# Expert rows of two mixture layers: loads before the last two experts, one-hot products for those two, transposes late in the products before

## The chip, the cores and the metric

The kernel runs on one core of a Trainium2 chip. The metric is the device time of one execution in microseconds (us). Three runs of the kernel before took 1920.16 to 1924.55 us, with a median of 1920.88 us.

## The reference, cut to what matters

The model is two blocks one after the other. The first is a state-space and attention block with a feed-forward part; the second has two layers, each a mixer (gated linear attention in layer 0, sparse attention in layer 1) followed by a mixture of experts. The change lies in the mixture of experts of both layers and in the layer normalization behind it:

```python
def moe_ffn(x, w_router, b_router, w_gate, w_up, w_down):
    ...
    s = jax.nn.sigmoid((xt @ w_router).astype(jnp.float32))
    ...
    _, top_e = lax.top_k(jnp.where(in_grp, biased, NEG), TOP_K)
    w = jnp.take_along_axis(s, top_e, axis=-1)
    w = w / jnp.sum(w, axis=-1, keepdims=True)
    gate = jnp.zeros((n, N_EXPERTS), jnp.float32).at[...].set(w)
    h = jax.nn.silu(jnp.einsum('nd,edf->nef', xt, w_gate)) * jnp.einsum('nd,edf->nef', xt, w_up)
    h = h * gate[:, :, None].astype(h.dtype)
    return jnp.einsum('nef,efd->nd', h, w_down).reshape(B, S, D)
...
    f = moe_ffn(x, moe_w_router, moe_b_router, moe_w_gate[i], moe_w_up[i], moe_w_down[i])
    x = layer_norm(DN_ALPHA * x + f, ln_g[i, 1], ln_b[i, 1])
```

There are 512 tokens of 1024 features, 16 experts with 256 hidden features each, and every token goes to two experts. Each expert has 3 MB of weights, so a layer reads 48 MB.

## The kernel before, in words

Tensors of tokens lie as four tiles of 128 tokens, xt[0] to xt[3], with 1024 features each. A product in nearly full precision is made as three products of halves (mm3, lines 393 to 396): every operand is split into a high part, cast on ScalarE, and the rest, subtracted on VectorE (split, line 368).

Weights come through one stream of 1 MB tiles (class Stream, lines 318 to 349). get asks for the load of a tile where the tile is used in program order, and rotates through a ring of buffers, ten (WM) in the expert layers. The framework then orders each engine's instructions by a simulated time line: a load whose buffer is free is issued long ahead of its use, in the order in which instructions become ready. An edge made by after (line 313) says that one instruction stands behind another on its engine, without a semaphore; Stream.later (line 341) gives every load of the stream such an edge behind the instruction st.behind, where that is set. All loads named here are issued by the queue of SyncE, SP, in which one that waits holds up what stands behind it.

```python
def ahead(self, n):
    for i in range(self.used, min(self.used + n, len(self.src))):
        if i not in self.tiles:
            ...
            ld = nc.sync.dma_start(out=t[:, :ap.shape[1]], in_=ap)
            self.later(ld)
def later(self, ld):
    if self.behind is not None:
        after(ld, self.behind)
def get(self):
    self.ahead(1)
```

Only project (line 1282) asks for ten tiles at once, before the experts begin. Of the 48 tiles of a layer the order is two of gate and up weights for expert e, then the one of down weights for expert e - 1.

The experts of a layer (experts, line 1463) run in a loop of 17 steps. Step e issues the gather of expert e + 1's rows from the DRAM copy xd of the tokens (gather, line 1423: an indirect DMA by GpSimd into one of three buffers xg, then eight transposes into PSUM tile xgt and a split into gh and gl, two buffers each), then the products of expert e with gate and up weights (up, line 1436: 24 matmuls into psh, two weight tiles), then those of expert e - 1 with its down weights (down, line 1445: two transposes ht, 12 matmuls into psy, one weight tile; ScalarE copies psy to SBUF, GpSimd scatters the rows to the DRAM tensor yd, one row for each token and choice).

combine (line 1480) follows. Eight loads of 512 KB bring yd back in the order of tokens, each behind all 16 scatters; st.behind is then set to the last of them. For each tile VectorE adds both choices, weighted (mac, line 1497, L1502), takes the statistics (L1512 to L1520), and ScalarE normalizes (L1173); done works on the tile before. In layer 0 done is x4_tile: transposes, split, and the products n with the weights w1, whose three tiles are split after the last psy is copied (line 1640). In layer 0 the first choice of tile 3 is weighted on ScalarE and added on GpSimd (aside). In layer 1 done is finish: gain and bias on GpSimd and VectorE and the store to the output. VectorE's order in this part is that of the program.

Of the kernel before, what the change touches and what calls it, by code (L numbers as in the profile page):

```python
# [10 lines left out]
F32 = mybir.dt.float32  # L11
FR = mybir.dt.float32r
F16 = mybir.dt.float16
# [6 lines left out]
P = 128  # L20
D = 1024
KD = 8
# [246 lines left out]
def build(ctx, tc, I, out, dbg=None):  # L269
# [123 lines left out]
    def mm3(o, a, b, start, stop):  # L393
        TE.matmul(o, a[0], b[0], start=start, stop=False)  # L394
        TE.matmul(o, a[0], b[1], start=False, stop=False)  # L395
        TE.matmul(o, a[1], b[0], start=False, stop=stop)  # L396

# [759 lines left out]
    def load_gb(gi):  # L1157
        gb = [sb(1024, n) for n in ("lng", "lnb")]
# [27 lines left out]
    class Layer:  # L1186
# [115 lines left out]
        def slots(self, q, idx):  # L1302

            psi = p1("inv")
            for i, (k, t) in enumerate(q):
                TE.matmul(psi[:, :32], q[k, t], self.rr[:, k, t], start=i == 0, stop=i == 7)
            return V.tensor_scalar(idx, psi[:, :32], float(2 * S), None, op0=ALU.add)

        def route(self, ts):
# [42 lines left out]
            self.idx = small("idx", (32,), I32)  # L1352
            wt.behind = self.slots(self.q, self.idx).ins.name

        def token_weights(self):
# [15 lines left out]
            V.reciprocal(wss, wss)  # L1371
            tt(self.wts, self.wts, wss.unsqueeze(1).to_broadcast([P, 2, 4]), ALU.mult)

        def overflow(self):

            top = nc.values_load(self.cnt[0:1, 0:1], min_val=0, max_val=S)
            with tc.If(top > CAP):
# [3 lines left out]
                with tc.For_i(1, S // P, 1):  # L1381
# [3 lines left out]
                    with tc.For_i(0, 16, 1) as e:  # L1385
# [27 lines left out]
                        for k in range(2):  # L1413
                            for nh in range(2):
# [3 lines left out]
                        A.copy(v2(yo), psy)  # L1418
                        G.indirect_dma_start(out=self.yd, out_offset=bass.IndirectOffsetOnAxis(ap=ie[:, 1:2], axis=0),
                                             in_=yo, in_offset=None, bounds_check=2 * S - 1, oob_is_err=False)  # L1420
            drop("oxg", "oxT", "ow", "ohs", "oyo", "qoh")

        def gather(self, e):
            xg = self.xg[e % 3]
            ld = G.indirect_dma_start(out=xg, out_offset=None, in_=self.xd, in_offset=bass.IndirectOffsetOnAxis(ap=self.idx[:, e:e + 1], axis=0),  # L1425
                                      bounds_check=S - 1, oob_is_err=False)
            if e == 0:
                st.hold = {st.used + WM + i: ld.ins.name for i in range(2)}
            ps = p2("xgt")
# [15 lines left out]
        def down(self, e, hs):  # L1445
# [10 lines left out]
            self.last = A.copy(v2(yo), psy).ins.name  # L1456
            s = G.indirect_dma_start(out=self.yd, out_offset=bass.IndirectOffsetOnAxis(ap=self.idx[:, 16 + e:17 + e], axis=0),
                                     in_=yo, in_offset=None, bounds_check=2 * S - 1, oob_is_err=False)
            for o in self.scat:
                tc.declare_no_dep(s.ins, o.ins, reason="rows of another expert's tokens")  # L1460
            self.scat.append(s)

        def experts(self):
            drop("zT", "lng", "lnb")
            wt.bufs = 4
            self.scat = []
            g, hs = {0: self.gather(0)}, {}
# [12 lines left out]
        def combine(self, done, aside):  # L1480

            ydv = self.yd.rearrange("(a k) d -> a k d", k=2)
            y2 = {}
            for t in range(4):
                for k in range(2):
                    y2[t, k] = sb(1024, "y2", bufs=8)
                    ld = nc.sync.dma_start(out=y2[t, k], in_=ydv[t * P:(t + 1) * P, k])
                    for s in self.scat:
                        tc.add_manual_dep(ld.ins, s.ins.name, mybir.DependencyInfo(mybir.DependencyClass.Sync, mybir.DependencyReason.DATA),
                                          reason="the rows of every expert")  # L1490
# [6 lines left out]
            def mac(t, k):  # L1497
                if k == 0 and t in aside:
                    A.activation(y2[t, 0], y2[t, 0], AF.Copy, scale=self.wts[:, 0, t:t + 1])
                    tt(xt[t], xt[t], y2[t, 0], ALU.add, G)  # L1500
                else:
                    V.scalar_tensor_tensor(xt[t], y2[t, k], self.wts[:, k, t:t + 1], xt[t], op0=ALU.mult, op1=ALU.add)  # L1502

            with tc.manual_schedule(engines={mybir.EngineType.DVE}):
                mac(0, 0)
                for t in range(5):
                    if t < 4:
                        z = xt[t]
                        mac(t, 1)
                        bs, mv, rs = (small(n, (w,), bufs=2) for n, w in (("bs", 12), ("mv", 2), ("lrs", 2)))  # L1510
# [12 lines left out]
                    if t < 4:  # L1523
                        normalize(z, z, rs)
            drop("y2")

# [81 lines left out]
    L0 = Layer(0)  # L1608
    L0.start()
    todo = [(f, b) for f in (gla_scores, gla_keys, gla_states) for b in range(4)]  # L1610
    for m in range(8):
# [63 lines left out]

    L0.combine(x4_tile, (3,))
    drop("x4f")
# [40 lines left out]
    for t in range(4):  # L1718
        affine(xt[t], L0.gb, V)
        dump(f'x4_{t}', xt[t])  # L1720
    drop("lng", "lnb")
    o = stream_tm(x4a)
# [200 lines left out]
    L1 = Layer(1)  # L1923
    L1.start()

    todo = [(i, [h]) for i in (3, 2) for h in range(16)] + [(i, [h, h + 1]) for i in (1, 0) for h in range(0, 16, 2)]
# [51 lines left out]
    def finish(t):  # L1978
# [4 lines left out]
        nc.sync.dma_start(out=out[t * P:(t + 1) * P, :], in_=xt[t])  # L1983
    L1.combine(finish, ())

# [15 lines left out]
```

## Time and profile before

| | us |
|---|---|
| median of three runs | 1920.88 |
| profiled execution, device time | 1918.51 |
| its span from first to last instruction | 1916.7 |
| layer 0: first gathered row transposed / last psy ends / layer's normalization begins | 1096.8 / 1255.9 / 1267.8 |
| layer 1: the same three | 1706.1 / 1871.7 / 1883.2 |

The span is counted from the first instruction; times in the rows are from there. PE is the matmul engine, DVE VectorE, ACT ScalarE, POOL GpSimd, SP the queue of loads and stores. In brackets behind an instruction stands how long its engine was idle before it and what ended that.

### The profile page before, as it was taken

The numbers are of one execution on the slowest core, as the hardware profiler recorded it, in microseconds if no ns is written. First come the engines' busy times: TensorE is split into PE (matmuls) and PEld (weight loads), VectorE is DVE, ScalarE is ACT, GpSimd is POOL, SyncE is SP. The second block draws the span as 40 slices with busy tenths as digits, with TensorE's granted clock in tenths as the row PEclk, the third lists the DMA queues.
The fourth block names the chain that finished last, engine by engine and source line by source line (L and its number), as shares of the span: only waits on it lengthen the run. The fifth ranks groups of instructions, "written<-read, shape, count | busy, mean of one in ns | idle before, by whom it ended". The sixth has DMA issues, their size and how long they took to land.

```text
span 1916.7 us, 27254 instructions
## 1 busy us (share of the span) xinstructions
PE 1743.3 (91%) x10719; PEld 1480.1 (77%) x10719; DVE 1221.8 (64%) x2276; ACT 874.1 (46%) x1397; POOL 173.3 (9%) x140
## 2 busy tenths in 40 slices
PE   8999999899999999999999799949998999859990
PEld 7899877798989988877888578738886777647870
DVE  7855368776555643253347889874337777669985
ACT  4233346433333332243223288843236665628881
POOL 2310000022000000000000122110000000012213
PEclk9999999899999999999999799979898999879995
DMA  5335221242322233212225599752230003539953
GB/s 194 110 110 140 89 88 65 63 160 90 108 89 89 88 135 114 95 66 88 88 88 206 188 325 380 281 217 77 85 136 23 1 12 123 208 126 338 380 224 140
DMA packets 69205, 269.73 MB, mean 141 GB/s; under 512 B 22144, under 2 KB 24720, under 8 KB 44240
## 3 DMA queue, kind: packets, MB, share of 16 engines
q1 hardware_dynamic: 52384, 246.38, 35.9%
q0 software_dynamic: 9216, 16.80, 2.4%
q10 hardware_dynamic: 7472, 4.76, 1.2%
q8 instruction: 85, 1.39, 0.3%
q14 instruction: 48, 0.39, 0.1%
HBM read 249.62 MB, written 30.43 MB: 146 GB/s over the span
## 4 chain that ended last, share of the span: by engine, by line
PE 63%; DVE 6%; ACT 3%; DMA 2%; issue 2%; POOL 0%; SPq 0%; POOLq 0%; DVEq 0%; ACTq 0%
PE mm L396 8%; PE mm L395 8%; PE mm L394 8%; PE psh L395 3%; PE psh L396 3%; PE psh L394 3%; PE tm L394 2%; PE tm L395 2%; PE tm L396 2%; PE npo L1920 2%; PE npt L1908 2%; PE op L395 2%; PE op L394 2%; PE op L396 2%; PE xgt L1431 1%
## 5 line engine op out<-in xcount | busy, mean ns | idle before, releaser
L369 ACT CAST pg<-pg 128x1024 fp32r<-128x1024 f32 (+2 forms) x437 | 427.4, 1007 | 554.1 <-PE mm L395 224.9
L369 DVE TENSOR_TENSOR pg<-pg,pg 128x1024 fp32r<-128x1024 f32 (+2 forms) x437 | 503.0, 1176 | 264.6 <-ACT pg L369 251.4
L396 PE MATMUL mm<-pg,pg 128*128 128x258 f32 (+2 forms) x1504 | 483.0, 322 | 4.0 <-DVE pg L369 4.0
L394 PE MATMUL mm<-pg,pg 128*128 128x258 f32 (+2 forms) x1504 | 484.9, 323 | 1.4 <-ACT pg L888 0.7
L395 PE MATMUL mm<-pg,pg 128*128 128x258 f32 (+2 forms) x1504 | 482.9, 321 | 0.0
L394 PEld LDWEIGHTS mm<-pg,pg 128*128 128x128 f32 x1504 | 287.6, 191 | 28.0 <-ACT pg L886 2.8
L396 PEld LDWEIGHTS mm<-pg,pg 128*128 128x128 f32 x1504 | 286.8, 191 | 24.9 <-DVE pg L369 4.7
L395 PEld LDWEIGHTS mm<-pg,pg 128*128 128x128 f32 x1504 | 287.4, 191 | 21.2 <-issue 0.4
L360 DVE TENSOR_TENSOR pg<-mm,pg 128x256 f32<-128x256 f32 (+3 forms) x138 | 66.2, 510 | 138.8 <-PE mm L396 138.8
L395 PE MATMUL psh<-pg,pg 128*128 128x512 f32 x256 | 106.4, 416 | 2.3 <-DVE pg L369 2.3
L394 PE MATMUL psh<-pg,pg 128*128 128x512 f32 x256 | 101.9, 398 | 0.0
L396 PE MATMUL psh<-pg,pg 128*128 128x512 f32 x256 | 101.3, 396 | 0.0
L394 PE MATMUL tm<-pg,pg 128*128 128x512 f32 x192 | 76.4, 408 | 4.6 <-ACT pg L1145 4.6
L395 PE MATMUL tm<-pg,pg 128*128 128x512 f32 x192 | 77.3, 403 | 1.2 <-DVE pg L369 1.2
L396 PE MATMUL tm<-pg,pg 128*128 128x512 f32 x192 | 76.1, 396 | 0.0
L360 DVE TENSOR_TENSOR pg<-pg,pg 128x512 f32<-128x512 f32 (+12 forms) x103 | 57.1, 575 | 24.9 <-ACT pg L675 10.6
L1892 ACT ACTIVATE pg<-ns,nmx 128x512 f32<-128x512 f32 (+3 forms) x128 | 66.3, 531 | 11.4 <-DVE nmx L1888 7.2
L1888 DVE TENSOR_REDUCE nmx<-ns 128x2 f32<-128x1024 f32 (+3 forms) x48 | 50.1, 1043 | 17.3 <-PE ns L1885 17.1
L360 DVE TENSOR_TENSOR pg<-pg 128x64 f32<-128x64 f32 (+8 forms) x127 | 49.5, 411 | 17.4 <-ACT pg L1033 15.4
L395 PEld LDWEIGHTS psh<-pg,pg 128*128 128x128 f32 x256 | 48.9, 191 | 13.2 <-DVE pg L369 4.4
L1425 POOL DMA_INDIRECT pg<-xd,idx x32 | 38.1, 1189 | 219.2 <-DVE wts L360 122.7
L394 PEld LDWEIGHTS psh<-pg,pg 128*128 128x128 f32 x256 | 48.8, 191 | 11.4
(440 smaller groups left out, 2960.9 us busy)
## 6 DMA issues: line engine op xcount, KB each, us to landing
pg<-in_w_moe_dram SPq DMA_DIRECT2D x96, 1024.0 KB, 10.4
pg<-in_w_up_dram SPq DMA_DIRECT2D x22, 1024.0 KB, 4.8
pg<-in_w_dn_dram SPq DMA_DIRECT2D x11, 1024.0 KB, 4.9
pg<-in_w_g_dram SPq DMA_DIRECT2D x8, 1024.0 KB, 5.5
pg<-in_w_go_dram SPq DMA_DIRECT2D x8, 1024.0 KB, 4.8
pg<-yd SPq DMA_DIRECT2D x16, 512.0 KB, 7.8
pg<-in_w_n_dram SPq DMA_DIRECT2D x8, 1024.0 KB, 6.8
pg<-in_w_no_dram SPq DMA_DIRECT2D x8, 1024.0 KB, 4.8
```

The costliest lines, as they stand in the source:

```text
L360: return (eng or V).tensor_tensor(o, a, b, op=op)
L369: return A.copy(h, src), V.tensor_tensor(l, src, h.bitcast(F32), op=ALU.subtract)
L394: TE.matmul(o, a[0], b[0], start=start, stop=False)
L395: TE.matmul(o, a[0], b[1], start=False, stop=False)
L396: TE.matmul(o, a[1], b[0], start=False, stop=stop)
L1425: ld = G.indirect_dma_start(out=xg, out_offset=None, in_=self.xd, in_offset=bass.IndirectOffsetOnAxis(ap=self.idx[:, e:e + 1], axis=0), bo ...
L1431: TE.transpose(ps[:, k // 4, (k % 4) * P:(k % 4 + 1) * P], xg[:, k * P:(k + 1) * P], ident)
L1888: V.tensor_reduce(mx, sc, axis=AX.X, op=ALU.max, negate=True)
L1892: A.activation(pp[:, r, br], sc[:, r, br], AF.Exp, bias=mx[:, r, br:br + 1], accum_out=se[:, r, br:br + 1])
L1908: TE.transpose(src[:, r, br, c * P:(c + 1) * P], pp[:, r, br, c * P:(c + 1) * P], ident)
L1920: TE.matmul(o_[64 * r:64 * r + 64], vsw[:, c * 512 + br * 256 + g * 64:c * 512 + br * 256 + (g + 1) * 64], pts[r][:, br, c * P:(c + 1) * P ...
```

## The change

- The gather and the transposes are parted. turn has the eight transposes; for expert e + 1 they stand, on PE, behind the 18th of the 24 matmuls of up(e).
- The rows of experts 0 to 13 are scattered as before. In step 14, behind down(13), four loads of 1 MB (both choices of 128 tokens each) bring yd back, each behind those 14 scatters, into the next four buffers of the weights' ring; st.behind is set to the last of them there. Eight mac instructions add them after the loop.
- Rows of yd that belong to experts 14 and 15 are zero: zd, a zeroed DRAM block, is copied over all of yd in eight DMAs for each layer.
- For experts 14 and 15 nothing is scattered. ScalarE scales their rows by the weight of the token in each row (sw, made in token_weights), VectorE makes four one-hot tiles for each (row's token against a ramp), and in combine four matmuls for each tile of tokens put the rows of both where they belong; VectorE adds them (add).

```diff
+    zd = dr.tile([P, 1024], F32, tag="zd", name="zd")
+    G.memset(xt[0], 0.0)
+    nc.sync.dma_start(out=zd, in_=xt[0])
...
+            self.tokf = small("tokf", (2,))
+            V.tensor_scalar(self.tokf, psi[:, 14:16], float(2 * S), None, op0=ALU.add)
...
+            tt(tl, self.oh[:, :, :, 14:], bc(self.wts, 2), ALU.mult)
+            V.tensor_scalar(w16[:, :, :, 0], tl, 4096.0, None, op0=ALU.mult)
...
+            for i, (k, t) in enumerate(self.q):
+                TE.matmul(psp[:, :6], self.q[k, t], w16[:, k, t].rearrange("p a e -> p (a e)"), start=i == 0, stop=i == 7)
+            self.sw = small("sw", (2,))
...
+        def zero(self):
+
+            for i in range(2 * S // P):
+                nc.sync.dma_start(out=self.yd[i * P:(i + 1) * P, :], in_=zd)
+
+        def load(self, t, y):
+            return nc.sync.dma_start(out=v2(y), in_=self.yd.rearrange("(a k) d -> a k d", k=2)[t * P:(t + 1) * P])
+
+        def mac(self, t, y):
+            for k in range(2):
+                V.scalar_tensor_tensor(xt[t], y[:, k * 1024:(k + 1) * 1024], self.wts[:, k, t:t + 1], xt[t], op0=ALU.mult, op1=ALU.add)
...
+        def turn(self, xg, behind=None):
+
             ps = p2("xgt")
             for k in range(KD):
-                TE.transpose(ps[:, k // 4, (k % 4) * P:(k % 4 + 1) * P], xg[:, k * P:(k + 1) * P], ident)
+                i = TE.transpose(ps[:, k // 4, (k % 4) * P:(k % 4 + 1) * P], xg[:, k * P:(k + 1) * P], ident)
+                if behind is not None:
+                    after(i, behind)
...
-                mm3(psh, (g[0][:, k * P:(k + 1) * P], g[1][:, k * P:(k + 1) * P]), wt.next(512), k == 0, k == KD - 1)
+                i = mm3(psh, (g[0][:, k * P:(k + 1) * P], g[1][:, k * P:(k + 1) * P]), wt.next(512), k == 0, k == KD - 1)
+                if k == 5:
+                    self.upto = i.ins.name
...
+            if e < 14:
+                A.copy(v2(yo), psy)
+                s = self.scatter(yo, self.idx[:, 16 + e:17 + e])
...
+                return
+
+            self.last = A.activation(v2(yo), psy, AF.Copy, scale=self.sw[:, e - 14:e - 13]).ins.name
+            m = self.xg[1][:, (e - 14) * 512:(e - 13) * 512]
+            for t in range(4):
+                V.tensor_scalar(m[:, t * P:(t + 1) * P], iota, float(t * P), self.tokf[:, e - 14:e - 13], op0=ALU.add, op1=ALU.is_equal)
+            self.late.append((m, yo))
...
             for e in range(17):
                 if e == 1:
                     wt.behind = None
                 if e < 15:
-                    g[e + 1] = self.gather(e + 1)
+                    xg[e + 1] = self.gather(e + 1)
                 if e < 16:
                     hs[e] = self.up(g.pop(e))
+                if e < 15:
+                    g[e + 1] = self.turn(xg.pop(e + 1), self.upto)
                 if e > 0:
                     self.down(e - 1, hs.pop(e - 1))
-            drop("xg", "gh", "gl", "hs", "hhl", "ysb", "wr", "wh", "wl")
+                if e == 14:
+                    for t in range(4):
+                        y.append(sb(2048, "wr", F32, WM))
+                        ld = self.load(t, y[t])
+                        for s in self.scat:
+                            tc.add_manual_dep(ld.ins, s.ins.name, mybir.DependencyInfo(mybir.DependencyClass.Sync, mybir.DependencyReason.DATA),
+                                              reason="the rows of every expert")
+                    st.behind = ld.ins.name
+            for t in range(4):
+                self.mac(t, y[t])
...
-            st.behind = ld.ins.name
...
+            def add(t):
+                ps = p2("late")
+                for nh in range(2):
+                    for i, (m, yo) in enumerate(self.late):
+                        TE.matmul(ps[:, nh], m[:, t * P:(t + 1) * P], yo[:, nh * 512:(nh + 1) * 512], start=i == 0, stop=i == 1)
+                tt(v2(xt[t]), v2(xt[t]), ps, ALU.add)
...
-                mac(0, 0)
+                add(0)
...
-                        mac(t, 1)
...
-                            mac(t + 1, 0)
+                            add(t + 1)
...
-    L0.combine(x4_tile, (3,))
+    L0.combine(x4_tile)
```

## Rows read from the trace of the kernel before

**Rows 1.** The page, its first part: busy time, share of the span, instructions.

```profile
PE 1743.3 (91%) x10719; PEld 1480.1 (77%) x10719; DVE 1221.8 (64%) x2276; ACT 874.1 (46%) x1397; POOL 173.3 (9%) x140
```

**Rows 2.** Windows: length, PE, PEld, DVE, ACT, POOL busy (count), clock, DMA share, GB/s.

```profile
820.00:870.00 50.00, 43.92 (x192) 32.76 (x191) 27.29 (x37) 25.21 (x21) 1.15 (x3) 0.94 0.20 71
...
1740.00:1820.00 80.00, 80.00 (x394) 66.02 (x393) 74.20 (x78) 69.14 (x85) 21.53 (x17) 1.00 0.97 369
...
1876.30:1889.00 12.70, 0.00 (x0) 0.00 (x0) 8.24 (x14) 1.53 (x2) 1.04 (x1) 0.50 0.90 328
```

**Rows 3.** Timeline of PE, layer 1: one expert's period, and a late wait.

```profile
1755.75 0.38 PE L1448 MATMUL ht<-c_ident,pg 128*128 128x128 f32 x2
...
1765.17 0.38 PE L1448 MATMUL ht<-c_ident,pg 128*128 128x128 f32 x2
...
1840.01 0.50 PE L395 MATMUL psh<-pg,pg 128*128 128x512 f32 x1 [0.51 <-DVE pg L369]
```

**Rows 4.** Timeline, layer 1, the first products: DVE, then PE.

```profile
1709.20 1.22 DVE L369 TENSOR_TENSOR pg<-xgt,pg 128x1024 fp32r<-128x1024 f32 x1 [3.63 <-ACT pg L369]
...
1714.95 1.97 PE L1431 MATMUL xgt<-c_ident,pg 128*128 128x128 f32 x8 [4.51 <-DMA pg<-xd,idx]
1716.57 0.78 PE L394 MATMUL psh<-pg,pg 128*128 128x512 f32 x1
...
1720.55 0.56 PE L394 MATMUL psh<-pg,pg 128*128 128x512 f32 x1
1720.95 0.39 PE L395 MATMUL psh<-pg,pg 128*128 128x512 f32 x1
1721.18 0.40 PE L396 MATMUL psh<-pg,pg 128*128 128x512 f32 x1
```

**Rows 5.** Timeline, layer 1, from the last product to the statistics.

```profile
1871.78 1.01 ACT L1456 COPY pg<-psy 128x1024 f32<-128x1024 f32 x1 [3.14 <-PE psy L396]
...
1873.07 0.97 POOL L1457 DMA_INDIRECT yd<-pg,idx  x1 [3.46 <-ACTq L1377]
...
1880.11 1.28 DVE L1502 SCALAR_TENSOR_TENSOR pg<-pg,wts,pg 128x1024 f32<-128x1024 f32 x1 [11.02 <-DMA pg<-yd]
...
1883.16 1.29 DVE L1512 BATCH_NORM_STATS2 bs<-pg 128x6 f32<-128x512 f32 x2
```

**Rows 6.** Timeline, layer 0, from the last product into the normalization.

```profile
1255.51 0.40 PE L396 MATMUL psy<-pg,pg 128*128 128x512 f32 x1
...
1258.48 4.96 DVE L369 TENSOR_TENSOR pg<-pg,pg 128x1680 fp32r<-128x1680 f32 x3 [5.22 <-ACT pg L369]
...
1267.80 1.29 DVE L1512 BATCH_NORM_STATS2 bs<-pg 128x6 f32<-128x512 f32 x2
...
1275.06 3.36 DVE L360 TENSOR_TENSOR pg<-pg,pg 128x1024 f32<-128x1024 f32 x1
```

**Rows 7.** Timeline of PE, layer 0, the first products.

```profile
1098.95 3.80 PE L1431 MATMUL xgt<-c_ident,pg 128*128 128x128 f32 x16 [0.18 <-DMA pg<-xd,idx]
```

**Rows 8.** SP's timeline around both layers' ends; time to landing of yd's DMAs.

```profile
1265.21 0.40 SPq L334 DMA_DIRECT2D pg<-in_w_n_dram  x1
...
1706.16 129.75 SPq L334 DMA_DIRECT2D pg<-in_w_moe_dram  x38
...
1876.33 3.93 SPq L1487 DMA_DIRECT2D pg<-yd  x8
...
DMA to landing us min/median/max: 3.1/6.3/10.6
```

**Rows 9.** Timeline of PE, layer 1: expert 15's products, and the last two of down.

```profile
1858.42 0.39 PE L394 MATMUL psh<-pg,pg 128*128 128x512 f32 x1
...
1864.34 0.40 PE L394 MATMUL psy<-pg,pg 128*128 128x512 f32 x1
...
1871.35 0.40 PE L396 MATMUL psy<-pg,pg 128*128 128x512 f32 x1
```

**Rows 10.** Timeline of PE, two whole f32 products of 512 columns (z).

```profile
831.13 1.02 PE L1100 MATMUL z<-pg,pg 128*128 128x512 f32 x2
```

More of the change, by code (lines that the diff above doesn't have):

```diff
@@ L395, in mm3 @@
         TE.matmul(o, a[0], b[1], start=False, stop=False)
-        TE.matmul(o, a[1], b[0], start=False, stop=stop)
+        return TE.matmul(o, a[1], b[0], start=False, stop=stop)
     def dense_fm(nk, x, cols, alloc=p2):
@@ L1157, in load_gb @@
     def load_gb(gi):
-        gb = [sb(1024, n) for n in ("lng", "lnb")]
+        g_ = sb(2048, "lngb")
+        gb = [g_[:, :1024], g_[:, 1024:]]
         for j in range(2):
@@ L1306, in slots @@
                 TE.matmul(psi[:, :32], q[k, t], self.rr[:, k, t], start=i == 0, stop=i == 7)
-            return V.tensor_scalar(idx, psi[:, :32], float(2 * S), None, op0=ALU.add)
+            return V.tensor_scalar(idx, psi[:, :32], float(2 * S), None, op0=ALU.add), psi
         def route(self, ts):
@@ L1352, in route @@
             self.idx = small("idx", (32,), I32)
-            wt.behind = self.slots(self.q, self.idx).ins.name
+            i, psi = self.slots(self.q, self.idx)
+            wt.behind = i.ins.name
+            self.tokf = small("tokf", (2,))
+            V.tensor_scalar(self.tokf, psi[:, 14:16], float(2 * S), None, op0=ALU.add)
         def token_weights(self):
@@ L1372, in token_weights @@
             tt(self.wts, self.wts, wss.unsqueeze(1).to_broadcast([P, 2, 4]), ALU.mult)
+            w16, tl = small("w16", (2, 4, 3, 2), F16), small("tl", (2, 4, 2))
+            tt(tl, self.oh[:, :, :, 14:], bc(self.wts, 2), ALU.mult)
+            V.tensor_scalar(w16[:, :, :, 0], tl, 4096.0, None, op0=ALU.mult)
+            V.scalar_tensor_tensor(tl, tl, 4096.0, w16[:, :, :, 0], op0=ALU.mult, op1=ALU.subtract)
+            V.tensor_copy(w16[:, :, :, 1], tl)
+            tt(w16[:, :, :, 2], tl, w16[:, :, :, 1], ALU.subtract)
+            for i, (k, t) in enumerate(self.q):
+                TE.matmul(psp[:, :6], self.q[k, t], w16[:, k, t].rearrange("p a e -> p (a e)"), start=i == 0, stop=i == 7)
+            self.sw = small("sw", (2,))
+            V.tensor_reduce(self.sw, psp[:, :6].rearrange("p (a e) -> p e a", a=3), axis=AX.X, op=ALU.add)
+            V.tensor_scalar(self.sw, self.sw, 1.0 / 4096, None, op0=ALU.mult)
         def overflow(self):
@@ L1418, in overflow, with scatter @@
                         A.copy(v2(yo), psy)
-                        G.indirect_dma_start(out=self.yd, out_offset=bass.IndirectOffsetOnAxis(ap=ie[:, 1:2], axis=0),
-                                             in_=yo, in_offset=None, bounds_check=2 * S - 1, oob_is_err=False)
-            drop("oxg", "oxT", "ow", "ohs", "oyo", "qoh")
+                        self.scatter(yo, ie[:, 1:2])
+                for t in range(4):
+                    nc.sync.dma_start(out=xt[t], in_=self.xd[t * P:(t + 1) * P, :])
+                    w = sb(2048, "ow")
+                    self.load(t, w)
+                    self.mac(t, w)
+            drop("oxg", "oxT", "ow", "ohs", "oyo", "qoh")
+        def scatter(self, yo, idx):
+            return G.indirect_dma_start(out=self.yd, out_offset=bass.IndirectOffsetOnAxis(ap=idx, axis=0),
+                                        in_=yo, in_offset=None, bounds_check=2 * S - 1, oob_is_err=False)
+        def zero(self):
[6 more added lines that the diff above has]
+                V.scalar_tensor_tensor(xt[t], y[:, k * 1024:(k + 1) * 1024], self.wts[:, k, t:t + 1], xt[t], op0=ALU.mult, op1=ALU.add)
         def gather(self, e):
@@ L1455, in down @@
             yo = sb(1024, "ysb", bufs=3)
[L1456 to L1461, printed above, removed]
+            if e < 14:
+                A.copy(v2(yo), psy)
+                s = self.scatter(yo, self.idx[:, 16 + e:17 + e])
+                for o in self.scat:
+                    tc.declare_no_dep(s.ins, o.ins, reason="rows of another expert's tokens")
+                self.scat.append(s)
+                return
[4 more added lines that the diff above has]
+            self.late.append((m, yo))
         def experts(self):
-            drop("zT", "lng", "lnb")
+            drop("zT", "lngb")
             wt.bufs = 4
-            self.scat = []
-            g, hs = {0: self.gather(0)}, {}
+            self.scat, self.late, y = [], [], []
+            xg = {0: self.gather(0)}
+            g, hs = {0: self.turn(xg.pop(0))}, {}
             for e in range(17):
@@ L1471, in experts @@
                 if e < 15:
-                    g[e + 1] = self.gather(e + 1)
+                    xg[e + 1] = self.gather(e + 1)
                 if e < 16:
                     hs[e] = self.up(g.pop(e))
+                if e < 15:
+                    g[e + 1] = self.turn(xg.pop(e + 1), self.upto)
                 if e > 0:
                     self.down(e - 1, hs.pop(e - 1))
-            drop("xg", "gh", "gl", "hs", "hhl", "ysb", "wr", "wh", "wl")
-            wt.bufs = 2
[L1480 to L1490, printed above, removed]
+                if e == 14:
[6 more added lines that the diff above has]
+                    st.behind = ld.ins.name
@@ L1491, in combine @@
+            for t in range(4):
+                self.mac(t, y[t])
+            drop("gh", "gl", "hs", "hhl", "wr", "wh", "wl")
+            wt.bufs = 2
+        def combine(self, done):
             self.gb = load_gb(2 * self.l + 1)
-            st.behind = ld.ins.name
             eps = small("epsl", (1,))
             V.memset(eps, LN_EPS / ALPHA ** 2)
[L1497 to L1502, printed above, removed]
+            def add(t):
[4 more added lines that the diff above has]
+                tt(v2(xt[t]), v2(xt[t]), ps, ALU.add)
@@ L1524, in combine @@
                         normalize(z, z, rs)
-            drop("y2")
+            drop("ysb", "xg")
     am, ket, states, held = [], [], {}, {}
@@ L1609, in build @@
     L0.start()
+    L0.zero()
     todo = [(f, b) for f in (gla_scores, gla_keys, gla_states) for b in range(4)]
@@ L1674, in x4_tile @@
         nc.sync.dma_start(out=kcd[t * P:(t + 1) * P, :], in_=s_)
-    L0.combine(x4_tile, (3,))
+    for _ in range(2):
+        sb(512, "kcv", bufs=2)
+    L0.combine(x4_tile)
     drop("x4f")
@@ L1720, in build @@
         dump(f'x4_{t}', xt[t])
-    drop("lng", "lnb")
+    drop("lngb")
     o = stream_tm(x4a)
@@ L1983, in finish @@
         nc.sync.dma_start(out=out[t * P:(t + 1) * P, :], in_=xt[t])
-    L1.combine(finish, ())
+    L1.combine(finish)
 def kernel(**inputs):
```

2 lines of the change are left out of this document (added).

## The prediction

> **What bounds the kernel now.** I read the busy times first: PE works 91% of the span [rows 1], so most of the time can only go where PE waits. Then the windows over the expert layers. In the steady middle of layer 1, PE is busy 80.00 of 80 us at full clock while the DMA engines are busy 97% and move 369 GB/s, and DVE works 74 of the 80 [rows 2]. An expert takes 9.42 us there, from one pair of ht transposes to the next [rows 3]. PE sets that pace; moving transposes about within it gains nothing, and a little more DMA or DVE work has not much room. The time that can be won lies at both ends of a layer. At its start PE waited 4.51 us for the gathered rows of expert 2, whose transposes stand ahead of expert 0's products although nothing of expert 0 needs them [rows 4]. At its end no PE instruction runs in the window while yd comes back [rows 2]: from the last psy (1871.75) to the first statistics (1883.16) 11.4 us pass in layer 1, in copy, scatter, load and two weighted adds [rows 5]; in layer 0 the same stretch is 1255.9 to 1267.8, 11.9 us [rows 6].
>
> **The change, part by part.** The sum is made against the profiled execution, 1918.51 us (span 1916.7 and 1.8 around it), which lies 2.4 us below the median of 1920.88.
>
> *Transposes late, first experts.* In layer 1 expert 0's products can begin when its own split is done: VectorE ends it at 1710.42 [rows 4], and the first two matmuls need only the high part, so PE starts at about 1709.2 instead of 1716.57: 7.4 us. The transposes of experts 1 and 2 now run within products, about 0.9 us each at full clock (the period of 9.42 us less 36 matmuls of 0.23 [rows 4] leaves 1.1 for them and ht): 1.8 us back. The slow stretch at half clock also costs a few more matmuls (ten at 0.43 us before the step to 0.23 [rows 4], some 13 now): 0.6. Layer 1 gains 5.0. In layer 0 expert 0's products waited only for 3.80 us of transposes, without a late gather [rows 7]; they could start some 2.5 earlier, 1.8 go back: 0.4 to 0.9, taken as 0.6.
>
> *Transposes late, all others.* Before, they came an expert early. Now the split must be done while PE has 6 matmuls of up and 12 of psy left, 18 x 0.23 = 4.2 us; cast 1.0 and subtraction 1.22 take 2.3 if neither engine is busy. No row shows this order. Nearest is the late wait of 0.51 us [rows 3], where a gathered tile's split pushed that of a weight back: bound above 0.75 us for each of some 13 experts in each layer, 10 a layer. Below, -0.4 a layer: the few late waits that vanish. I take -0.4, since 4.2 us is nearly twice the 2.3 that are needed.
>
> *Row loads in step 14, and what stands behind them.* The four loads wait for the scatter of expert 13, and st.behind is set there, with four tiles of the layer's weights not yet asked for: two of up(15), one each of down(14) and down(15) (step 14 ends at tile 44 of 48, and get asks for one tile at its use). They get an edge behind the last row load, so on SP they can't go before it. That such an edge holds is seen in layer 0, where a load of the stream goes out at 1265.21, right behind the row loads [rows 8]. Before, all 38 were out by 1835.9 [rows 8], 22 us ahead of expert 15. Now: psy(13) ends where psh of expert 15 begins, at 1858.4 (up to the start, not counting the gain above) [rows 9]. Copy 1.0 and its launch 0.2; POOL starts the scatter 0.3 later, SP's first load follows 3.26 after that start [rows 5, 8]: 1863.2. Four MB of rows took 12.7 us to move [rows 2]; the time to landing grew along them from 3.1 to 10.6 us [rows 8], so a transfer waits behind those before it. 1875.9. The first weight tile needs 2.8 more (1.05 MB at 369 GB/s [rows 2]), its cast 1.0: expert 15's first matmul at 1879.8 instead of 1858.42. That is 21.4 us in which PE has nothing to do. Its clock will have fallen to half (0.50 in a window without PE work [rows 2]), and the first two chunks are split with PE waiting: about 2.2 more up to the last psy. In sum +23.6 in each layer. Bounds: 14, if weights share the bandwidth with the rows instead of waiting behind them; 27, if the gain and bias loads (1 MB) go between as well.
>
> *The end of a layer.* Rows are then long landed: the eight mac (1.28 each [rows 5]) fall into PE's idle stretch and cost nothing; were the weights in time, they would end some 7 us behind the last psy. Behind the last psy: scaled copy 1.0 instead of the plain one, launch 0.1, two products of the last expert, one tt of 1.2 (as the split from PSUM). Two whole f32 products of 512 columns took 1.02 us [rows 10]. So the statistics begin some 3.6 us behind the last psy: -7.8 in layer 1, -8.3 in layer 0. In each of three further tiles one mac of 1.28 is gone from DVE's chain, the other is replaced by an add of the same length: -3.8 a layer. The rest of the 16 products lies in DVE's shadow.
>
> Of f32 products the Trainium skill, FP8 and Floating Point Precision, section TensorE Precision Notes, says that a true FP32 product takes four passes through the array. By that two products would take about 1.9 us and the sum would be 0.9 us higher in each layer; the 1.02 us [rows 10] do not bear it out.
>
> *Layer 0 alone.* aside goes: its add on GpSimd drew a tt on DVE out to 3.36 us [rows 6], 2.1 longer than the usual 1.2: -2.1. The splits of w1, 4.96 us on DVE, stood in an idle stretch [rows 6]; their loads now come behind the weights, the splits between the products and the adds, where DVE has about half of that time idle: +2.5.
>
> *Small things.* token_weights has about eight tiny DVE instructions and eight products more; they lie in the 3.63 us in which DVE waited before its first gathered split [rows 4]. Eight masks of 128 columns (some 1.6 us) lie in PE's idle stretch. Zero rows are 8 DMAs a layer, 8.4 MB in all, without a wait on any late data: at 369 GB/s 23 us of all DMA engines. SP may issue them as soon as zd is there, ahead of stream tiles; the ring's lead would hide most of that. Bounds 0 and 23 us; I take 0, as the DMA engines are busy only 20% where layer 0 begins [rows 2].
>
> **Sum.** Layer 1: +23.6 - 7.8 - 3.8 - 5.0 - 0.4 = +6.6. Layer 0: +23.6 - 8.3 - 3.8 - 2.1 + 2.5 - 0.6 - 0.4 = +10.9. Together +17.5 us: 1936.0, of which I make 1937 as the median lies higher.
>
> **Rivals.**
> - *The last four weight tiles are not held.* Were they out before the row loads, PE would run through as before. Then the two +23.6 fall away. Rows then land until 4.2 us behind the last psy; if all mac go first, the last end at 6.8 and the statistics begin at 8.0 instead of 3.6, 4.4 later in each layer. Sum between -21 and -30: 1889 to 1898. For it: before, weights were always far ahead. Against it: the order of the code and the edge that held [rows 8]. It decides at one point, whether loads of in_w_moe follow those of yd on SP. Chance 0.15.
> - *Weights share the way with the rows.* The order holds, but the tiles land along with the rows, 9.6 us sooner in each layer (the lower bound of 14): 1917. Against it: landing times that grow along the queue [rows 8]. Chance 0.08.
> - *Splits too late for PE in every expert.* Price 0.75 x 26 = 20 us on top: 1957. For it: DVE's 74 of 80 us [rows 2]. Chance 0.09.
> - *Zero rows hold up the stream of weights.* Up to 23 us on top, most likely some 10: 1947. Chance 0.05.
> - The forecast as it stands: 0.63, 1925 to 1948 by the bounds of its terms.
>
> **How the numbers follow.** Measured differences below 0.3% (5.8 us) can't be told from none. Faster: the first rival and a little of the second and of the forecast: 0.17. Within 0.3%: most of the second rival and the forecast's lower edge: 0.09. Slower: 0.74. The range 1914 to 1956 leaves out the first rival and the upper end of the third, under 0.2 together.
>
> **What would show it.** In the changed trace the last four loads of in_w_moe of each layer must stand behind those of yd on SP, and PE must show an idle stretch of about 20 us before the first psh of expert 15, ended by a split of a weight. The first psh of layer 1 must begin some 3 us behind the first xgt, without a wait for the gather of expert 2. From the last psy to the first statistics there should be 3 to 4 us. The period in the middle must stay 9.4 us. The forecast is wrong if PE runs through from expert 13 to 15, or if the loads of weights stay ahead of those of yd.

## The result and the profile after

The changed kernel takes 1953.88 us (median of 4 runs, 1948.78 to 1956.36) against 1922.72 us in the runs beside it. The ratio is 1.0156, 95% interval 1.0132 to 1.018: some 31 us slower. The forecast was 1937, from a sum of +17.5 us. The sign is right and the time lies in the range, but the loss is nearly twice what the sum gave.

The profiled execution of after took 1948.78 us with a span of 1947.0, 30.3 more than before's. The page's busy row and the windows answer to [rows 1, 2]; the columns are the same.

```profile
PE 1771.4 (91%) x10799; PEld 1489.4 (76%) x10799; DVE 1234.8 (63%) x2317; ACT 877.7 (45%) x1396; POOL 160.3 (8%) x136
```

```profile
1760.00:1840.00 80.00, 80.00 (x392) 65.79 (x391) 73.39 (x77) 71.21 (x86) 18.77 (x17) 1.00 1.00 375
1242.50:1263.40 20.90, 0.13 (x1) 0.00 (x0) 10.01 (x8) 1.99 (x3) 0.98 (x1) 0.62 0.74 299
1874.20:1894.70 20.50, 0.04 (x1) 0.00 (x0) 10.04 (x8) 2.04 (x3) 0.97 (x1) 0.62 0.76 307
```

The middle of a layer is unchanged: PE busy 80 of 80 us. What is new is a stretch of some 20 us in each layer with no work on PE, between expert 13's and expert 15's products. The timelines of SP, ACT and PE there (layer 0, then SP and PE in layer 1) show who is waited for:

```profile
1247.79 1.97 SPq L1456 DMA_DIRECT2D pg<-yd  x4
1249.86 1.93 SPq L334 DMA_DIRECT2D pg<-in_w_moe_dram  x4
...
1262.42 1.99 ACT L369 CAST pg<-pg 128x1024 fp32r<-128x1024 f32 x2 [18.74 <-DMA pg<-in_w_moe_dram]
...
1263.51 0.79 PE L394 MATMUL psh<-pg,pg 128*128 128x512 f32 x1 [20.88 <-ACT pg L369]
...
1878.96 1.97 SPq L1456 DMA_DIRECT2D pg<-yd  x4
1881.03 1.89 SPq L334 DMA_DIRECT2D pg<-in_w_moe_dram  x4
...
1894.76 0.80 PE L394 MATMUL psh<-pg,pg 128*128 128x512 f32 x1 [20.52 <-ACT pg L369]
```

The last four weight loads stand behind the four row loads, ACT waits for them and PE for ACT, as forecast. The rest is in the table: each layer cut at the first xgt, the end of psy(13), the end of the last psy, the first statistics, and the fourth statistics (layer 0) or the end of the span (layer 1). The times are starts and ends of instructions in the two timelines; the forecast column holds the terms on record.

| stretch | layer 0: before, after | change | forecast | layer 1: before, after | change | forecast |
|---|---|---|---|---|---|---|
| first xgt to end of psy(13) | 145.8, 148.1 | +2.3 | -1.0 | 152.3, 149.8 | -2.5 | -5.4 |
| to end of last psy | 13.3, 37.1 | +23.8 | +23.6 | 13.3, 36.8 | +23.4 | +23.6 |
| to first statistics | 11.9, 8.7 | -3.2 | -5.8 | 11.4, 5.6 | -5.8 | -7.8 |
| to fourth statistics, or end | 29.2, 24.6 | -4.6 | -5.9 | 33.5, 30.4 | -3.1 | -3.8 |
| sum | | +18.3 | +10.9 | | +12.0 | +6.6 |

(In layer 0, -5.8 is -8.3 and the +2.5 of w1's splits; -5.9 is -3.8 and -2.1.) Outside these stretches the differences are -2.3 ahead of layer 0's experts and +2.2 between the layers. So the stall was sized to 0.2 us, and every gain came out too small, the first stretch most of all.

Two groups of rows show the shortfalls. The front of layer 1 (PE, then ACT, then PE), which answers to [rows 4]:

```profile
1724.41 1.97 PE L1474 MATMUL xgt<-c_ident,pg 128*128 128x128 f32 x8 [6.09 <-DMA pg<-xd,idx]
...
1727.48 0.79 PE L394 MATMUL psh<-pg,pg 128*128 128x512 f32 x1 [0.91 <-ACT pg L369]
...
1735.35 0.40 PE L396 MATMUL psh<-pg,pg 128*128 128x512 f32 x1
1735.58 1.04 PE L1474 MATMUL xgt<-c_ident,pg 128*128 128x128 f32 x8
...
1735.46 1.28 ACT L1488 ACT_TABLE_LOAD   x1
1736.76 0.38 ACT L1488 ACTIVATE pg<-psh 128x256 f32<-128x256 f32 x1
1737.04 1.04 ACT L369 CAST pg<-pg 128x1024 fp32r<-128x1024 f32 x1
1737.97 1.02 ACT L369 CAST pg<-xgt 128x1024 fp32r<-128x1024 f32 x1
...
1739.04 0.70 PE L394 MATMUL psh<-pg,pg 128*128 128x512 f32 x1 [2.42 <-ACT pg L369]
```

Expert 0's products begin 3.1 us behind the first xgt, as forecast; before it was 10.4. But expert 1's first product waits 2.42 us for its cast, which stands on ACT behind a table load, a silu and a weight cast. The same wait is in layer 0 at 1108.45. The product at 1735.35 is the 24th and last of expert 0's up: the edge lets expert 1's transposes start behind the 18th, but on PE they stand behind all 24. So it is in both layers of all six kernels that have them late. And the ends: in layer 1 the add of the first tile waits for PE's late products, in layer 0 two of w1's splits stand ahead of it and the third behind it. First PE, ACT and DVE in layer 1, then DVE in layer 0:

```profile
1910.83 1.88 PE L1557 MATMUL late<-pg,pg 128*128 128x512 f32 x4
1912.54 1.02 PE L1557 MATMUL late<-pg 128*128 128x512 f32 x2
1913.40 1.02 PE L1557 MATMUL late<-pg,pg 128*128 128x512 f32 x2
1914.26 1.88 PE L1557 MATMUL late<-pg 128*128 128x512 f32 x4
...
1911.03 1.11 ACT L1511 ACTIVATE pg<-psy,sw 128x1024 f32<-128x1024 f32 x1 [3.59 <-PE psy L396]
...
1915.32 1.22 DVE L360 TENSOR_TENSOR pg<-pg,late 128x1024 f32<-128x1024 f32 x1 [7.42 <-PE late L1557]
1916.58 0.69 DVE L1567 BATCH_NORM_STATS2 bs<-pg 128x6 f32<-128x512 f32 x1
```

```profile
1282.37 3.14 DVE L369 TENSOR_TENSOR pg<-pg,pg 128x1680 fp32r<-128x1680 f32 x2 [5.81 <-ACT pg L369]
1285.43 1.22 DVE L360 TENSOR_TENSOR pg<-pg,late 128x1024 f32<-128x1024 f32 x1
1286.56 1.90 DVE L369 TENSOR_TENSOR pg<-pg,pg 128x1680 fp32r<-128x1680 f32 x1
1288.38 1.28 DVE L1567 BATCH_NORM_STATS2 bs<-pg 128x6 f32<-128x512 f32 x2
```

### The profile page after: what moved, and what is told of

The parts are those of the page before. It is cut to its first block, busy times and chain, and to the rows that moved or that the text cites. A ratio compares the mean times of both kernels' runs of the same rounds, so it can differ in the third digit from the quotient of the medians.

```text
span 1947.0 us, 27434 instructions
## 1 busy us (share of the span) xinstructions
PE 1771.4 (91%) x10799; PEld 1489.4 (76%) x10799; DVE 1234.8 (63%) x2317; ACT 877.7 (45%) x1396; POOL 160.3 (8%) x136
## 5 line engine op out<-in xcount | busy, mean ns | idle before, releaser
L394 PE MATMUL psh<-pg,pg 128*128 128x512 f32 x256 | 106.6, 417 | 48.1 <-ACT pg L369 48.1
L395 PE MATMUL psh<-pg,pg 128*128 128x512 f32 x256 | 106.4, 416 | 1.3 <-DVE pg L369 1.2
L396 PE MATMUL psh<-pg,pg 128*128 128x512 f32 x256 | 104.3, 407 | 0.6 <-DVE pg L369 0.5
L394 PEld LDWEIGHTS psh<-pg,pg 128*128 128x128 f32 x256 | 50.4, 197 | 59.9 <-ACT pg L369 49.6
L1950 ACT ACTIVATE pg<-ns,nmx 128x512 f32<-128x512 f32 (+3 forms) x128 | 66.3, 531 | 10.5 <-DVE nmx L1946 7.3
L395 PEld LDWEIGHTS psh<-pg,pg 128*128 128x128 f32 x256 | 50.1, 196 | 13.5 <-DVE pg L369 3.0
L396 PEld LDWEIGHTS psh<-pg,pg 128*128 128x128 f32 x256 | 49.9, 195 | 12.9 <-DVE pg L369 2.6
```

Source lines behind the costliest of these rows:

```text
L396: return TE.matmul(o, a[1], b[0], start=False, stop=stop)
L1950: A.activation(pp[:, r, br], sc[:, r, br], AF.Exp, bias=mx[:, r, br:br + 1], accum_out=se[:, r, br:br + 1])
```

## The experiments

A caution for all of them: the code ahead of layer 0's experts is nearly the same everywhere, yet in the twelve profiled executions their first xgt starts between 1092.6 and 1102.5 us. A difference of 5 us between two medians is therefore read together with the stretches of the table, which don't contain that.

**The weights not held (e1_free).**

```diff
-                    st.behind = ld.ins.name      # in step 14
+            st.behind = ld.ins.name              # after the loop
             for t in range(4):
                 self.mac(t, y[t])
 # load_gb: the loads go through st.later(...)
```

> The changed kernel with one thing undone: the edge behind the last row load is set after the loop, so the last four weight tiles of each layer are free to go ahead of the rows (the gain and bias loads get the edge instead, so that they don't go between). Theory (the traces of before and after side by side): the held weights cost 23.4 to 23.8 us in each layer between the end of psy(13) and the end of the last psy. With them free PE runs through from expert 13 to 15, those 47 us go, and the rows, which then land until some 4 us behind the last psy, give 2 to 4 us a layer back: about 1910 us (1904 to 1916), a little faster than before. Rival 1, bandwidth: rows and weights move at the same time and PE still waits, some 10 us a layer: about 1930. Rival 2: the idle stretch only covered another bound (VectorE's weighted adds, which then stand ahead of the weight splits): 1935 or more, with PE waiting for VectorE at expert 15.

Measured: 1927.84 us (10 runs), ratio to before 1.0016, interval 1.0002 to 1.003. The stretch from psy(13) to the last psy falls from 37.1 to 17.1 us in layer 0 and from 36.8 to 16.2 in layer 1. So the held weights are the stall: 40.6 us of it go when the edge is set later. Against before, 3.8 and 2.9 us are left. But 1910 was a miss. ACT and PE in layer 0, then DVE:

```profile
1253.37 1.01 ACT L1504 COPY pg<-psy 128x1024 f32<-128x1024 f32 x1 [1.76 <-PE psy L396]
1254.28 1.99 ACT L369 CAST pg<-pg 128x1024 fp32r<-128x1024 f32 x2
...
1255.38 0.79 PE L394 MATMUL psh<-pg,pg 128*128 128x512 f32 x1 [2.05 <-ACT pg L369]
```

```profile
1267.73 10.15 DVE L1460 SCALAR_TENSOR_TENSOR pg<-pg,wts,pg 128x1024 f32<-128x1024 f32 x8
1278.10 3.14 DVE L369 TENSOR_TENSOR pg<-pg,pg 128x1680 fp32r<-128x1680 f32 x2 [0.21 <-DVEq L1396]
1281.16 1.21 DVE L360 TENSOR_TENSOR pg<-pg,late 128x1024 f32<-128x1024 f32 x1
1282.40 1.29 DVE L1567 BATCH_NORM_STATS2 bs<-pg 128x6 f32<-128x512 f32 x2
...
1285.54 1.91 DVE L369 TENSOR_TENSOR pg<-pg,pg 128x1680 fp32r<-128x1680 f32 x1 [0.52 <-ACT pg L369]
```

The eight weighted adds had been free because PE stood idle beside them; now they start 2.7 us ahead of the last psy's end (1270.5) and fill, with two of w1's splits, 10.5 of the 11.9 us from there to the first statistics, and the third split comes late. The table's third row is 3.3 longer in each layer than in after, the fourth 5.6 in layer 0: 40.6 - 12.2 = 28.4 us, against 26.0 between the medians. Rival 1 gave nearly this time (1930), but not for this reason: PE loses 3.8 and 2.9 us a layer and not 10, and what it waits for (2.05) is a cast that stands on ScalarE behind expert 13's copy, not a load. Rival 2 was half right: VectorE is the next bound, at the end though and not at expert 15.

**Expert 1's transposes free (e2_first); the late transposes alone (e3_late_only); both (c4).**

```diff
 # e2_first: in after.  c4: the same line in e3_late_only
-                    g[e + 1] = self.turn(xg.pop(e + 1), self.upto)
+                    g[e + 1] = self.turn(xg.pop(e + 1), self.upto if e else None)
```

e3_late_only is the kernel before with the gather and turn of after (`turn` called behind `up`, its transposes behind `self.upto`) and nothing else.

> The changed kernel, but the transposes of expert 1 alone are free to run before expert 0's products (all later experts stay late). Theory: in both layers PE waited 2.4 us for expert 1's split, because its transposes come so late that ScalarE's cast is not done in the half-clock stretch; that wait goes and some 0.9 us of transposes moves ahead: 1.5 to 2.4 us less in each layer, 3 to 5 in all, about 1950 us against 1954. Rival: the first products are slow for the low clock alone, and the wait only moves to expert 0 or 2: no change, 1954.

> The kernel before with the late transposes and nothing else of the change. Prediction on record: layer 1 gains 5.0, layer 0 0.6, few late waits less 0.8: 6.4 us faster, about 1916 against 1922. Theory now, from the trace of after: 2.5 of the gain in layer 1 is given back by the wait of expert 1, layer 0 gains nothing or loses 2: between 3 us faster and 0, about 1920. Rival (splits too late in every expert): up to 10 us slower in each layer, which would show as a period over 9.5 us.

> The kernel before with the late transposes alone, expert 1's left free (the one with all late measured 1921.7 us against 1923.1 of before). Theory: late transposes are worth 5.0 + 0.6 us as the prediction had it once expert 1's, which have only six products and no psy between them and their use, are not late: 1915 to 1918 us, a ratio of 0.996 to 0.9975. Rival: psh of expert 0 waits for expert 1's gather instead, and the late splits of the other experts cost what is won: 1922, no change.

Measured: e2_first 1943.51 us, ratio 1.0096 (1.0066 to 1.0126), 10 us less than after, where 3 to 5 were expected. e3_late_only 1921.69 us, ratio 1.0002 (0.9987 to 1.0017): no change. c4 1912.89 us, ratio 0.9953 (0.9937 to 0.997): faster, and by more than was expected. The first stretch of the table, in the kernels with expert 1's transposes late (after and those labelled e1, e3, e4, e5, e6) and in those with them free (e2, c1, c3, c4; c2 stands apart, see there):

| | layer 0 | layer 1 |
|---|---|---|
| before | 145.8 | 152.3 |
| late, six kernels | 148.1 to 152.2 | 148.3 to 149.8 |
| free, four kernels | 145.5 to 145.8 | 144.4 to 146.5 |

So the late transposes of expert 1 alone cost 2.3 us or more in layer 0 and 1.8 or more in layer 1, by the means of the rows 4.5 and 3.6. In the pairs that differ in this line alone it is 2.3 and 3.6 (after and e2_first), 5.2 and 5.3 (e3_late_only and c4); the rest of e2_first's 10 us lies in no stretch of its profiled execution. By the means that is more than the wait of 2.4. Windows behind it show a part of the reason: of after in layer 0 and layer 1, then of e6 in layer 0, and last of e2 in layer 1, where there is no such wait.

```profile
1111.00:1114.00 3.00, 3.00 (x15) 2.44 (x14) 1.61 (x2) 2.18 (x3) 0.00 (x0) 1.00 0.80 284
...
1740.00:1743.00 3.00, 3.00 (x10) 2.20 (x9) 0.89 (x2) 0.74 (x2) 0.00 (x0) 0.57 0.86 277
```

```profile
1116.00:1119.00 3.00, 3.00 (x9) 2.32 (x8) 1.23 (x1) 1.04 (x1) 0.00 (x0) 0.50 0.70 254
```

```profile
1741.00:1744.00 3.00, 3.00 (x19) 2.54 (x18) 2.53 (x3) 3.00 (x4) 0.00 (x0) 1.00 0.80 287
```

The granted clock (third number from the right) falls to half behind the wait in two of these stretches and stays at 1.00 in one, with the same wait of 2.42 to 2.43 us ahead of all three. In layer 0 the period from expert 0's ht to expert 1's is 10.2 us in after and 13.1 in e6, most of the spread from 148.1 to 152.2. With expert 1 free, late transposes keep in sum what the prediction promised: in c4 the first stretch is 7.9 shorter than before in layer 1 (5.4 promised), but only 0.1 in layer 0 (1.0 promised).

**The late products in two parts (e4_fr).** Rows of experts 14 and 15 are split into yh and yl, each multiplied by the one-hot mask in the weights' type.

```diff
-            self.last = A.activation(v2(yo), psy, AF.Copy, scale=self.sw[...]).ins.name
+            self.last = A.activation(v2(yh), psy, AF.Copy, scale=sw).ins.name
+            V.scalar_tensor_tensor(v2(yl), psy, sw, v2(yh).bitcast(F32), op0=ALU.mult, op1=ALU.subtract)
...
-            self.late.append((m, yo))
+            self.late += [(m, yh), (m, yl)]
```

> The changed kernel with the one-hot products of the last two experts in two parts, as the weights have it: rows split into a high and a low part, two products of 0.23 us in place of one f32 product. Theory: one f32 product of 512 columns takes 0.86 us (two records of 0.43), so four of them 3.4 us for each tile; eight of 0.23 take 1.8. The statistics then begin 1.6 to 2 us earlier in each layer, and in layer 0 the adds of later tiles wait less: 3 to 6 us less in all, 1948 to 1951 against 1954, although VectorE has one subtraction of 1.2 us more for each of the two experts. Rival (the prediction): the products lie in VectorE's shadow and only the subtraction counts: 0 to 2 us slower.

Measured: 1948.45 us, ratio 1.0135 (1.0102 to 1.0169), overlapping after's. The median moved as the theory said, but not where it said: from the last psy to the first statistics it is 8.7 and 5.2 us (after 8.7 and 5.6), and to the fourth 24.7 (24.6). In layer 1:

```profile
1910.87 1.28 DVE L1513 SCALAR_TENSOR_TENSOR pg<-psy,sw,pg 128x1024 fp32r<-128x1024 f32 x1 [3.83 <-ACT pg L1512]
1913.68 1.22 DVE L360 TENSOR_TENSOR pg<-pg,late 128x1024 f32<-128x1024 f32 x1 [1.52 <-PE late L1559]
```

The add now waits 1.52 us behind the subtraction for products, and the subtraction of 1.28 stands ahead of them: what the products give, it takes. The rival holds on the path; the 5 us lie in other stretches, inside the spread.

**w1's splits behind the first statistics (e5_w1), zero rows twice (e6_zero2).**

```diff
 # e5_w1: combine(done, between), in the loop
+                    if t == 0 and between is not None:
+                        between()               # the three splits of w1
 # e6_zero2: L0.zero() and L1.zero() are called twice
```

> The changed kernel with one thing moved: the three splits of w1 stand on VectorE behind the first statistics' chain and no longer between the weighted adds and the first add of the one-hot products. Theory: of the 8.7 us from layer 0's last psy to its first statistics, some 2.5 to 3 are these splits; the first product of the next stage needs w1 later, so 1.5 to 3 us go: 1951 to 1952. Rival: the first statistics wait for TensorE's f32 products anyway (7.42 us in layer 1): no change, 1954.

> The changed kernel with each layer's zero rows written twice (8 more DMAs of 0.5 MB a layer). Prediction on record: zero rows cost nothing, so twice costs nothing: within 3 us of 1954. Rival (they hold up the stream of weights, up to 23 us for 8.4 MB): 5 to 20 us more.

Measured: e5_w1 1955.79 us, ratio 1.0179 (1.0142 to 1.0216), overlapping after's. In layer 0 the first statistics come 5.6 us behind the last psy instead of 8.7, and the fourth 31.2 behind the first instead of 24.6: what leaves the front of the chain is paid twice inside it. Neither the theory nor its rival said so. e6_zero2 1953.06 us, ratio 1.015 (1.0115 to 1.0186): 8 more DMAs a layer cost nothing that can be seen, which fits the 0 of the prediction. Leaving the zero rows out was not tried, since rows would be read that nothing wrote.

**Several at once (c1, c2, c3).** c1 is e1_free and e2_first, with the four weight tiles asked for ahead of the rows:

```diff
                 if e == 14:
+                    st.ahead(4)
                     for t in range(4):
                         y.append(sb(2048, "wr", F32, WM))
```

> The changed kernel with two parts undone at once: the last four weight tiles are asked for ahead of the row loads (they also get their places in the ring ahead of them), and expert 1's transposes are free. Theory (costs add): from the kernel with free weights, 1928 us, the 2.3 and 3.7 us of expert 1 go, and the wait of 2 us with its half-clock stretch before expert 15, some 4 a layer, goes too, since the weight splits now stand ahead of expert 13's copy; but that copy, and so the rows, come some 2 to 3 us later: 1916 us (1910 to 1921), a little faster than before. Rival (the end is bound by the rows, not by PE): what PE gains before expert 15 is lost to the later rows, 1922, the same as before.

> As the one with two parts undone, and the end put in order: rows of the last experts split in two parts for cheap products; of the weighted adds only tile 0's and 1's before the statistics, tile 2's and 3's in the shadow of later square roots; the splits of w1 behind the first statistics; expert 15's hidden cast ahead of expert 14's scaled copy. Theory: VectorE's queue between the last psy and the first statistics (eight weighted adds of 1.27, three splits of 5 us in layer 0) was what was left there, 9 to 12 us; it shrinks to 4 to 6 us, and about half of that is given back where the moved instructions lie in the chain of later tiles: 3 to 5 us less in each layer, about 1909 us (1903 to 1915). Rival: VectorE works without a gap from the first statistics to the end of a layer, so what is moved behind them is lost again: no faster than the kernel it comes from.

Measured: c1 1921.46 us, ratio 0.9987 (0.9967 to 1.0007); c2 1927.05 us, ratio 1.0027 (1.0008 to 1.0047). Both expectations (1916 and 1909) were missed. In c1 PE runs through: 13.8 us from psy(13) to the last psy in both layers, 13.3 before. But in layer 0 it then takes 15.2 us to the first statistics and 32.5 on to the fourth. SP, ACT and DVE of c1:

```profile
1256.74 0.33 SPq L334 DMA_DIRECT2D pg<-in_w_n_dram  x1
1260.45 1.65 SPq L1164 DMA_DIRECT2D pg<-in_lngb_dram  x2
...
1263.60 1.59 ACT L369 CAST pg<-pg 128x1680 fp32r<-128x1680 f32 x1 [7.54 <-SPq L1396]
...
1275.80 1.91 DVE L369 TENSOR_TENSOR pg<-pg,pg 128x1680 fp32r<-128x1680 f32 x1 [3.09 <-ACT pg L369]
```

The gain and bias loads wait for a page that still holds rows (SP's waits show 2.4 us for the weighted adds there), SP reaches the branch (L1396) late, and ACT's cast of w1 waits at that branch for SP. In c2, which takes the products in two parts as well and moves tile 2's and 3's weighted adds and w1's splits behind the first statistics, the first statistics come 8.4 and 3.6 us sooner than in c1, and the fourth 8.0 and 10.4 later behind them: what was moved is lost again, as its rival said. VectorE is full there in layer 1 (23.0 of 23.9 us) but not in layer 0 (30.2 of 40.4), so what bounds layer 0 there is not shown. Its first stretches also grew (149.0 and 148.8), where the first products waited for other instructions of DVE and ACT.

c3 takes c1 and frees that queue instead:

```diff
+            ar.rings.update(wr=(4, ring[:-4]), y=(4, ring[-4:]))   # rows keep their pages
...
+        def gain_bias(self):                                       # called behind w1's loads
+            self.gb = load_gb(2 * self.l + 1)
+            drop("y")
...
+            if e == 14:
+                after(j, self.c13)      # ht's cast, and up(15)'s later splits: behind expert 13's copy
```

> From the one with two parts undone (1921.5 us): the rows keep their own places until the gain and bias of the next normalisation and the three tiles of w1 have theirs, so that SyncE's queue no longer waits for the weighted adds before the branch; and expert 13's copy goes ahead of the later weight splits, so that the rows are asked for some 2 us sooner. Theory: in layer 0 the third split of w1 (3.1 us waited, 1.9 worked, between the first and the second statistics) and about 1 us at the branch in each layer go, and the weighted adds begin 1 to 2 us sooner: 4 to 8 us less, about 1915 us (1912 to 1918), faster than before by a little. Rival (VectorE has no gap left from the rows to the end): the same as before, 1921.

Measured: 1906.32 us (6 runs, 1904.1 to 1913.45), ratio 0.9931 (0.9909 to 0.9953): faster than both kernels, and more than was expected. SP and DVE of c3, layer 0:

```profile
1249.79 1.28 SPq L334 DMA_DIRECT2D pg<-in_w_n_dram  x3
1251.12 0.99 SPq L1164 DMA_DIRECT2D pg<-in_lngb_dram  x2
...
1251.14 10.15 DVE L1464 SCALAR_TENSOR_TENSOR pg<-pg,wts,pg 128x1024 f32<-128x1024 f32 x8
1262.24 3.90 DVE L369 TENSOR_TENSOR pg<-pg,pg 128x1680 fp32r<-128x1680 f32 x2 [0.94 <-ACTq L1396]
```

The w1 tiles and the gain and bias are all asked for by 1252 (in c1 the second tile went out at 1256.74, the gain and bias at 1260.45, the third tile behind the branch), the weighted adds start at 1251.14 instead of 1254.11, and the stretch to the fourth statistics is 26.5 instead of 32.5 us; in layer 1 the first statistics come 9.2 us behind the last psy instead of 11.6. With 0.9 in layer 1's first stretch that explains 9.3 of the 15 us by which c3 beats c1; 6 more lie between the layers, inside the spread. c4's interval overlaps c3's, so which of the two is better stays open.

## Why the prediction was right or wrong

*The stall: right, in place and size.* +23.6 was written, +23.8 and +23.4 measured, with the order on SP and the waits as described, and e1_free removes 20 us of it in each layer. That it fits to 0.2 us is luck in part: PE's wait was put at 21.4 us and took 20.9 and 20.5, the slow products behind it at 2.2 and took 2.9. The first rival's condition (weights ahead of rows) did not hold; where the experiments made it hold, its price was wrong: it gave 1889 to 1898, e1_free measured 1927.84 and c1 1921.46. It counted the eight adds (8.0 us from the last psy to the statistics; e1_free has 8.9 in layer 1, but 11.9 in layer 0), and left out that w1's splits come out of their cover with them and that rows then sit on pages that the next loads want. The rest it shares with the forecast, whose gains below were too large.

*Transposes late: the step that failed.* The prediction gave "18 x 0.23 = 4.2 us" between a late transpose and its use: 6 products of up and 12 of psy. For expert 1 none of the 18 stands between. Expert 0's down comes behind it, and the transposes stand behind all 24 products of up (1735.58), so nothing is left to cover a split that the same paragraph puts at 2.3 us. The result is the wait of 2.42 us and, behind it, half clock in some stretches. Of the 2.42 us, 1.35 pass while ACT is still at a table load (1.28 us), a silu and a weight's cast, and the rest is the cast itself. Why the transposes come so late on PE, when the edge allowed six products sooner, no run shows. The range covered lateness in every steady expert, which did not happen (the period is 9.43 us, 9.42 in [rows 3]; the bound of 0.75 us for it stands on no row), and not this one expert. The term was -1.0 in layer 0 and -5.4 in layer 1 and came out at +2.3 and -2.5: 3.3 and 2.9 us, about half of what the forecast lacked (12.8 us). Freeing expert 1's transposes alone gives 2.3 and 3.6 of it back (e2_first).

*The end of a layer: right in kind, 2.6 us too good in layer 0 and 2.0 in layer 1.* In layer 1, 3.6 us were forecast from the last psy to the statistics (the parts named there add up to 3.3), 5.6 measured. The scaled copy is as forecast (1.11); between its end at 1912.1 and the add at 1915.32 PE works through f32 products that start 0.86 us apart, where the prediction had two in 1.02. In layer 0 the splits of w1 were put "where DVE has about half of that time idle", +2.5; two of them (3.14) stand ahead of the first add and the third (1.90) between it and the statistics, 5.0 in all.

*The f32 products: a row misread.* [rows 10] has two records; L1100 issues 4 products and leaves 8 records, and the late products, 16 a layer, leave 64 in all. So one product of 512 columns is two records, 0.86 us by the starts above, against 0.23 for one product of the weights' type [rows 4]. The prediction turned down what the Trainium skill says in FP8 and Floating Point Precision, TensorE Precision Notes, that a true FP32 product takes four passes. The ratio of 3.7 agrees with it.

*Smaller terms.* The later tiles gained 4.6 and 3.1 where 5.9 and 3.8 stood: the mac less is real, and in layer 0 one later add waits 2.66 us for late products (at 1304.26); where the 0.7 of layer 1 went is not shown. Zero rows cost nothing that can be seen, as taken. The masks and token_weights don't show. The 3.1 us of [rows 8] is a scatter's landing; the row loads took 3.8 to 10.6 us, growing along the queue as the prediction had it, so its sum is not touched.

## What to carry to other kernels

An edge that orders a stream behind something holds every load not yet asked for: at the place where it is set, count how many loads those are and how soon the first is needed. Where an operation is moved to just in time, count what stands between it and its use in the first round too, not in the steady one alone. Work that hides in a stall is not free: before the stall is removed, price what comes out from under it.

## What was not expected of the hardware

The same wait of 2.4 us on PE was followed by full clock in one execution and by half clock in others, in the same place of the same code (1.00 against 0.50 in layer 0), which makes such a wait cost from 2.4 to some 5 us (the periods of 10.2 and 13.1). A function change on ScalarE took 1.28 us in the first silu of a layer; the Trainium skill, in ScalarE activation tables: per-element evaluation and per-set limits, section What a function is on this engine, gives 1283 ns for it, which the row bears out. And the program ahead of layer 0's experts varied by 10 us between the twelve executions, more than most single effects studied here.
